# Moving the LayerNorm's scale and shift, and the weight rests, from GpSimd to VectorE in a two-block network

## The chip, the cores and the metric

The kernel runs on one core of a Trainium2 chip as one program with one launch. Its time is the time on the device in microseconds (us); lower is better. Before the change it is 3112.41 us, the median of three runs (3110.68 to 3112.63). A core has five engines that each work through their own queue in order: TensorE (PE in the profile; its weight loads are PEld), VectorE (DVE), ScalarE (ACT), GpSimd (POOL), and SyncE (SP), which issues most of the DMAs.

## The reference

512 tokens of 1024 channels pass through two blocks. The first, in which the change lies, has two layers, and each layer three sublayers, each closed by a LayerNorm over a residual sum:

```python
for l in range(DEPTH):                                  # DEPTH = 2
    h = 0.5 * _swiglu(x, ffn_w_gate[l, 0], ffn_w_up[l, 0], ffn_w_down[l, 0])
    x = _layernorm(ALPHA * x + h, ln_g[l, 0], ln_b[l, 0])
    h = _mixer(x, w_in[l], ...)
    x = _layernorm(ALPHA * x + h, ln_g[l, 1], ln_b[l, 1])
    h = 0.5 * _swiglu(x, ffn_w_gate[l, 1], ffn_w_up[l, 1], ffn_w_down[l, 1])
    x = _layernorm(ALPHA * x + h, ln_g[l, 2], ln_b[l, 2])
# _layernorm: (x - mean) * rsqrt(var + 1e-5) * g + b
# _swiglu:    (silu(x @ wg) * (x @ wu)) @ wd, width 2816
# _mixer:     x @ w_in, then a causal convolution of 31 taps with its own LayerNorm, a gated linear
#             recurrence, and attention in a window with a bias per relative position; then @ w_out
```

The second block (a state-space scan, a gating unit, and 16 routed experts) is not touched by the change.

## The kernel before, in words

**Numbers in split passes.** A product of two float32 matrices is made of three passes of a rounded type: high times high, high times low, low times high (`mm3`, lines 115 to 119). A weight unit of 128 x 1024 is therefore loaded into a ring of four raw buffers, rounded by ScalarE (line 82, tile `whl`), and its rest, raw minus rounded, is computed by a second engine (line 83). This document calls that instruction a rest. The ring of split units has seven places; a place comes free when TensorE has used its unit. Which engine computes a rest is told by `pool_lo`: in the three feed-forward stages after the first it is GpSimd for the first 6 units, in a mixer GpSimd for all 14 units of the input projection, and VectorE everywhere else.

**Stages.** The first block is six stages in a row, numbered from 0: feed-forward, mixer, feed-forward, and the same again. A stage projects its input (`proj`, 24 matmuls for 128 output columns), does its own work, and projects back in `down`. The tokens are four tiles `x[0]` to `x[3]` of 128 x 1024, and `down` works by halves of two tiles: the products of the second half lag five units behind those of the first, so that the LayerNorm of the first half can run beside the last products of the second.

**The boundary of two stages** is the end of `down` (lines 228 to 268). `ln_stats` forms the residual sum on VectorE (line 133), the squares and the root on ScalarE (lines 137 and 138), and normalizes on VectorE (line 141). The normalized tile is transposed by TensorE into PSUM (`transposes`, tile `tb`), and `evac_T` brings it back: ScalarE applies the LayerNorm's scale and shift, which on the transposed side are one number for each partition (line 160, tile `y`), VectorE rounds (line 162, tile `xTh`) and forms the rest (line 163, tile `xTl`). There are four such pairs for each half. Then TensorE projects the first four units of the next stage for the first half of the tokens (tile `pj`), with the transposes of `x[2]` and `x[3]` between them, and the next stage begins with the same units for the second half.

**The residual copy.** The tiles `x[t]` themselves, which the next LayerNorm needs again, are normalized but not yet scaled. `gb_apply` (lines 172 to 176) multiplies and adds on GpSimd with the scale and shift spread over all partitions (tile `gb`), two instructions for each tile, at the boundary. After the last stage another routine, `gb_halves`, does this, by halves on VectorE and GpSimd.

**The mixer** has VectorE run 62 taps of the convolution (tile `acc`, line 362), which are queued behind the projections' own work; the low part of each query (`ql`, line 396) is formed on the same engine, and TensorE needs it for the scores (`sc`, line 451). The bias band of the attention (tile `bias`) shares its one buffer with `gb`, and is loaded at the mixer's start by a DMA that GpSimd issues (line 610). GpSimd also does six products of the recurrence (lines 427 to 431).

**Order.** The program is written in one order, and a scheduler then orders each engine's queue by its own priorities and estimates. The places of instructions are told below from the built program.

Of the kernel before, what the change touches and what calls it, by code (L numbers as in the profile page):

```python
# [13 lines left out]
D = 1024  # L14
# [17 lines left out]
NPOOL = 6  # L32
# [7 lines left out]
class Stream:  # L40
    """Weight units, in the order the tensor engine takes them: loaded ahead into a ring,
    then (where a product runs in split passes) parted into a rounded and a rest."""
# [25 lines left out]
    def ensure(self, n):  # L68
        k = self.k
        while self.n_split < min(n, self.limit or len(self.units)):  # L70
# [6 lines left out]
            if self.units[i][1]:  # L77
                r = self.raw.pop(i)
                w = r.shape[-1]
                t = k.splitp.tile([128, 2, 1024], F32R, tag="hl", name="whl")  # L80
                hi, lo = t[:, 0, :w], t[:, 1, :w]
                k.nc.scalar.activation(hi, r, AF.Copy)  # L82
                k.lo_engine(i).tensor_tensor(out=lo, in0=r, in1=hi.bitcast(F32), op=OP.subtract)  # L83
                self.hl[i] = (hi, lo)
                self.load_to(i + 1 + RAWS)
# [14 lines left out]
class Kernel:  # L100
    def __init__(self, tc, a, out):
        self.tc, self.nc, self.a, self.out = tc, tc.nc, a, out
        self.bg = []

    def lo_engine(self, i):
        return self.nc.gpsimd if i in self.pool_lo else self.nc.vector

# [64 lines left out]
    def gb_apply(self, t):  # L172
        g, b = self.gb
        eng = self.nc.gpsimd
        eng.tensor_tensor(out=self.x[t], in0=self.x[t], in1=g, op=OP.mult)
        eng.tensor_tensor(out=self.x[t], in0=self.x[t], in1=b, op=OP.add)
# [20 lines left out]
    def down(self, u0, n, lhs, ln, nxt, at=None, pace=4):  # L197
        """lhs(u, half): the split stationary operand of unit u for a half of the tokens.
        nxt: a projection follows; its first units run for each half by itself."""
# [29 lines left out]
        g, b = self.ln_cols(ln)  # L229
        rest = [lhs(u, 1) for u in range(n - LAG, n)]  # L230
# [5 lines left out]
        for s in range(LAG):  # L236
# [5 lines left out]
            if s == LAG - TB:  # L242
                if nxt:
                    self.transposes(1, self.x[1], tb)
                    self.evac_T(0, tb, g, b)
                    self.gb_apply(0)
                    self.gb_apply(1)
# [10 lines left out]
        for i in range(4):  # L258
# [4 lines left out]
            if i == T3:  # L263
                self.transposes(3, self.x[3], tb)
                self.evac_T(1, tb, g, b)
                self.gb_apply(2)
                self.gb_apply(3)
# [7 lines left out]
    def ffn(self, st, pb, ln, nxt, setup=None, at=None, views=()):  # L275
# [4 lines left out]
        def post(f, pg, pu):  # L280
# [3 lines left out]
            nc.vector.scalar_tensor_tensor(h, sg, 0.5, pu, op0=OP.mult, op1=OP.mult)  # L284
            hs[f] = h

# [19 lines left out]
        for f in range(NF):  # L306
# [12 lines left out]
            post(f, pg, pu)  # L319
# [7 lines left out]
    def mixer(self, l, st, pb, ln, nxt):  # L327
# [26 lines left out]
        def tap(c, j):  # L354
            """Tap j of the causal convolution: its input reaches j tokens back."""
# [10 lines left out]
        def post_xb(c):  # L366
# [4 lines left out]
            for j in range(1, LTAPS):  # L371
                nc.vector.scalar_tensor_tensor(t[:, j:], b[:, :T - j], wj(j), t[:, j:], op0=OP.mult, op1=OP.add)
            xc.append(t)

# [169 lines left out]
        for c in range(2):  # L544
            pj(4 + c)
            post_xb(c)
        for c in range(2):
            pj(6 + c)
            self.drain(4)
        for c in range(2):  # L550
# [48 lines left out]
    def mixer_tiles(self, l, mp):  # L599
# [6 lines left out]
        self.kl = mp.tile([128, T], F32R, name="kl")  # L606
        self.bias = self.gbp.tile([128, 4, 2, 256], F32, tag="gb", name="bias")
# [9 lines left out]
    def setup(self):  # L617
# [9 lines left out]
        self.eps5 = self.cp1.tile([128, 1], F32, name="eps5")  # L627
# [9 lines left out]
    def lru_consts(self, pool):  # L637
        """8 log sigmoid(lambda) of each channel, and its negative."""
# [10 lines left out]
    def log1p_exp_neg_abs(self, pool, v, n):  # L649
        """log(1 + exp(-|v|)) by 2 atanh(e / (2 + e)), e = exp(-|v|)."""  # L650
# [17 lines left out]
    def band_bias(self, pool):  # L668
        """The additive band [query, r, g, key], -1e30 outside the window, from rel_bias."""
# [43 lines left out]
def chan(v, n):  # L713
    """[..., n*128] vectors as columns [128, ... * n]"""
# [4 lines left out]
def layout1(i):  # L719
# [9 lines left out]
    # natural q tile (2g + r//2), half r%2  ->  tile r holds (g, d)  # L729
# [44 lines left out]
class Carve:  # L774
    """Small tiles out of larger ones that are not in use yet."""
# [18 lines left out]
class Program(Kernel):  # L794
# [53 lines left out]
    def mod_cols(self):  # L848
        """shift and scale (lat, ctx) as columns; the scale with norm1's weight."""
# [38 lines left out]
    def xm_half(self, half, rs):  # L888
        """The modulated norm of two token tiles, transposed and split."""
# [17 lines left out]
    def ctx_stats(self):  # L907
        """The rms norm's factor of each token of the context, along a row, for all partitions."""
# [16 lines left out]
    def ctx_split(self):  # L925
        """The modulated norm of the context, transposed and split."""
# [22 lines left out]
    def proj2(self, i, bank, src, cols, every=0):  # L949
        """128 output channels for the columns cols of the split operand src."""  # L950
# [8 lines left out]
    def spread(self):  # L959
        """Some of the waiting steps, so that they end with the last of the places for them."""  # L960
# [62 lines left out]
    def conv3(self, bank, n, i, dst):  # L1023
        """Centred three-tap convolution with bias, then silu."""
# [8 lines left out]
    def grp_main(self, pool, g, u, ready={}):  # L1033
        """B, x (2 tiles) and C of a group: projection, convolution."""
# [27 lines left out]
    def grp_p1(self, pool, g, G):  # L1062
        """The states and the combined decay of a group, as steps to spread."""
# [60 lines left out]
        def step(dst, src, c, d, p):  # L1124
            """dst = src * chunk decay + state"""
# [115 lines left out]
    def norm_ss(self):  # L1241
        """The groups' rms norm of the scan's output."""
# [11 lines left out]
    def v_half(self, u, half):  # L1254
        """Natural projection of half of v's channels, with gelu, into the tokens' tiles."""
# [66 lines left out]
    def post(self, outer, U, xd):  # L1322
        nc, tc, w, a = self.nc, self.tc, self.w, self.a
        with ExitStack() as es:
# [86 lines left out]
            # h = x + merged @ (w_o * g1)  # L1411
# [583 lines left out]
```

## Time and profile before

| what | value |
|---|---|
| median of three runs | 3112.41 us |
| the profiled execution: span from first to last instruction | 3109.9 us |
| granted clock of TensorE over the span (1.0 is 2.4 GHz, 0.5 is 1.2 GHz) | 0.978 |
| TensorE busy | 2980.0 us, 96% |
| VectorE busy | 1347.5 us, 43% |
| ScalarE busy | 1000.7 us, 32% |
| GpSimd busy | 410.0 us, 13% |

The profile is one execution. A row of the timeline reads: start, duration, engine, line, operation, output and input with sizes, count, and in brackets how long the engine had stood idle and which engine and instruction it then had waited for. The rows give no time of their own for the run beside the span, which is 2.5 us under the median of the runs. The first block takes some 1960 us of the span, and its five boundaries lie at about 380, 587, 972, 1366 and 1574 us.

### The profile page before, as it was taken

To read this page: it belongs to the slowest core of one execution; us is meant where nothing else is said; L and a number is where in the kernel's file an instruction comes from. 1 tells how busy PE (TensorE), PEld (TensorE's weight loads), DVE (VectorE), ACT (ScalarE), POOL (GpSimd) and SP (SyncE) were. 2 spreads that over 40 slices of the span, in tenths; PEclk is the share of its full clock that TensorE was granted. 3 is DMA by queue.
4 is the path that set the end of the run, shared out by engine and by line. 5 is a ranking of instruction groups with operands and counts; after the bars stand their busy time and mean duration, and the time that the engine had idled before them with its cause. 6 is when DMAs were issued, how large, how long until landed. Compare 5 with 4: busy or idle time off the path is not lost.

```text
span 3109.9 us, 35375 instructions
## 1 busy us (share of the span) xinstructions
PE 2980.0 (96%) x14404; PEld 2241.7 (72%) x14404; DVE 1347.5 (43%) x2068; ACT 1000.7 (32%) x1583; POOL 410.0 (13%) x259
## 2 busy tenths in 40 slices
PE   8999998899998999989889999999999999999998
PEld 7888774788887878877578888878788884444443
DVE  4223468532335233357552234788773441211112
ACT  4223335322223222234543223577542221000002
POOL 0000341400004000053040000133230110000000
PEclk9999998899999999989999999999999999999999
DMA  6432324233322353222533323222433368999994
GB/s 192 113 95 82 95 78 153 88 106 98 95 77 87 106 192 106 81 84 70 167 115 95 95 82 97 90 95 82 139 127 95 95 252 330 360 379 379 379 369 176
DMA packets 127747, 465.91 MB, mean 150 GB/s; under 512 B 12901, under 2 KB 13429, under 8 KB 126560
## 3 DMA queue, kind: packets, MB, share of 16 engines
q1 hardware_dynamic: 119488, 435.81, 40.3%
q0 software_dynamic: 6656, 23.12, 2.6%
q10 hardware_dynamic: 1440, 4.72, 0.4%
q8 instruction: 113, 1.85, 0.3%
q14 instruction: 50, 0.41, 0.0%
HBM read 457.71 MB, written 5.88 MB: 149 GB/s over the span
## 4 chain that ended last, share of the span: by engine, by line
PE 84%; DVE 11%; DMA 2%; ACT 1%; POOL 1%; issue 1%; SPq 0%; DVEq 0%; ACTq 0%; POOLq 0%
PE dn L215 18%; PE pg L117 6%; PE pg L119 6%; PE pg L118 6%; PE pu L117 5%; PE pu L119 5%; PE pu L118 5%; PE ey L1674 4%; PE eg L1674 4%; PE eu L1674 4%; DVE acc L362 3%; PE pj L118 2%; PE ga L1661 2%; PE pj L119 2%; PE pj L117 2%; DVE xTl L163 2%
## 5 line engine op out<-in xcount | busy, mean ns | idle before, releaser
L83 DVE TENSOR_TENSOR whl<-raw,whl 128x1024 fp32r<-128x1024 f32 x339 | 430.5, 1274 | 669.0 <-ACT whl L82 668.2
L82 ACT ACTIVATE whl<-raw 128x1024 fp32r<-128x1024 f32 (+1 forms) x385 | 405.9, 1056 | 665.1 <-PE pu L119 238.1
L215 PE MATMUL dn<-whl,hhl 128*128 128x512 f32 x2112 | 495.0, 396 | 0.0
L215 PEld LDWEIGHTS dn<-whl,hhl 128*128 128x128 f32 x2112 | 396.6, 188 | 95.1
L117 PE MATMUL pg<-xTh,whl 128*128 128x512 f32 x768 | 300.2, 391 | 0.0
L119 PE MATMUL pg<-xTh,whl 128*128 128x512 f32 x768 | 299.0, 389 | 0.0
L118 PE MATMUL pg<-xTl,whl 128*128 128x512 f32 x768 | 298.9, 389 | 0.0
L117 PE MATMUL pu<-xTh,whl 128*128 128x512 f32 x704 | 274.6, 390 | 0.0
L119 PE MATMUL pu<-xTh,whl 128*128 128x512 f32 x704 | 273.9, 389 | 0.0
L118 PE MATMUL pu<-xTl,whl 128*128 128x512 f32 x704 | 273.9, 389 | 0.0
L118 PE MATMUL pj<-xTl,whl 128*128 128x256 f32 (+1 forms) x688 | 238.1, 346 | 32.2 <-DVE xTl L163 31.9
L117 PE MATMUL pj<-xTh,whl 128*128 128x256 f32 (+1 forms) x688 | 243.3, 354 | 21.7 <-DVE xTh L162 21.7
L83 POOL TENSOR_TENSOR whl<-raw,whl 128x1024 fp32r<-128x1024 f32 x46 | 113.1, 2465 | 925.7 <-ACT whl L82 925.6
L119 PE MATMUL pj<-xTh,whl 128*128 128x256 f32 (+1 forms) x688 | 233.9, 340 | 0.0
L118 PEld LDWEIGHTS pj<-xTl,whl 128*128 128x128 f32 x688 | 141.4, 206 | 49.1 <-DVE xTl L163 38.3
L117 PEld LDWEIGHTS pg<-xTh,whl 128*128 128x128 f32 x768 | 144.1, 188 | 36.6 <-issue 7.4
L117 PEld LDWEIGHTS pj<-xTh,whl 128*128 128x128 f32 x688 | 141.3, 205 | 36.3 <-DVE xTh L162 25.8
L119 PEld LDWEIGHTS pg<-xTh,whl 128*128 128x128 f32 x768 | 144.2, 188 | 30.0
L118 PEld LDWEIGHTS pg<-xTl,whl 128*128 128x128 f32 x768 | 144.3, 188 | 29.6
L1674 PE MATMUL eu<-er,xg 128*64 128x512 f32 x512 | 160.1, 594 | 0.0
L1674 PE MATMUL eg<-er,xg 128*64 128x512 f32 x512 | 152.9, 596 | 0.0
L119 PEld LDWEIGHTS pu<-xTh,whl 128*128 128x128 f32 x704 | 132.1, 188 | 27.7
(476 smaller groups left out, 4239.2 us busy)
## 6 DMA issues: line engine op xcount, KB each, us to landing
raw<-in_wgu SPq DMA_DIRECT2D x176, 512.0 KB, 3.5
er<-in_eu SPq DMA_DIRECT2D x64, 1024.0 KB, 10.0
er<-in_eg SPq DMA_DIRECT2D x64, 1024.0 KB, 9.8
er<-in_ed SPq DMA_DIRECT2D x56, 1024.0 KB, 7.4
raw<-in_wd SPq DMA_DIRECT2D x88, 512.0 KB, 3.5
raw<-in_win SPq DMA_DIRECT2D x76, 512.0 KB, 3.5
raw<-in_ada_w SPq DMA_DIRECT2D x48, 512.0 KB, 4.1
raw<-in_wout SPq DMA_DIRECT2D x16, 512.0 KB, 4.6
```

The lines of the kernel that those rows point to most:

```text
L82: k.nc.scalar.activation(hi, r, AF.Copy)
L83: k.lo_engine(i).tensor_tensor(out=lo, in0=r, in1=hi.bitcast(F32), op=OP.subtract)
L117: mm(out, l[0], r[0], start=start, stop=False)
L118: mm(out, l[0], r[1], start=False, stop=False)
L119: mm(out, l[1], r[0], start=False, stop=stop)
L163: nc.vector.tensor_tensor(out=lo, in0=y, in1=hi.bitcast(F32), op=OP.subtract)
L215: nc.tensor.matmul(banks[t, dh], l[:, s], r[:, dh * 512:(dh + 1) * 512], start=(u == 0 and n_l == 0), stop=(u == last and n_l == 2))
L362: nc.vector.scalar_tensor_tensor(acc[:, j:], y[:, :T - j], wj, acc[:, j:], op0=OP.mult, op1=OP.add)
L1661: nc.tensor.matmul(src, self.x[t][:, k * 128:k * 128 + 128], G[:, t], start=(t == 0), stop=(t == 3))
L1674: nc.tensor.matmul(banks[dh][r * 64:r * 64 + 64], l(k, r), ws[r][:, j, dh * 512:(dh + 1) * 512], start=(first and j == 0), stop=(last and ...
```

## The change

The scale and shift of the residual copy leave the boundary. `down` now only lists them, eight instructions for four tiles, and `gb_later` takes them from the list in the next stage and puts them on VectorE, each behind an instruction that it is given: in a feed-forward stage one for each step from the third, in a mixer two behind each of four places. All rests go to VectorE; `pool_lo` and `NPOOL` are gone. The bias band, which shares a buffer with the scale and shift, is loaded behind them. And a root of a one-number tile is placed in `down` ahead of the last part, so that ScalarE's table for the root is loaded there. Comments and docstrings were cut in the same edit, which moves line numbers only.

```diff
@@ Stream.ensure
-                k.lo_engine(i).tensor_tensor(out=lo, in0=r, in1=hi.bitcast(F32), op=OP.subtract)
+                k.nc.vector.tensor_tensor(out=lo, in0=r, in1=hi.bitcast(F32), op=OP.subtract)
...
-    def gb_apply(self, t):
-        g, b = self.gb
-        eng = self.nc.gpsimd
-        eng.tensor_tensor(out=self.x[t], in0=self.x[t], in1=g, op=OP.mult)
-        eng.tensor_tensor(out=self.x[t], in0=self.x[t], in1=b, op=OP.add)
+    def gb_later(self, n, ins):
+
+        with self.tc.issue_after(ins.ins):
+            for t, v, op in self.gb_todo[:n]:
+                self.nc.vector.tensor_tensor(out=self.x[t], in0=self.x[t], in1=v, op=op)
+        self.gb_todo = self.gb_todo[n:]
...
@@ down
         g, b = self.ln_cols(ln)
+        self.tc.keep_in_program_order(nc.scalar.activation(self.table, self.eps5, AF.Sqrt))
...
                     self.evac_T(0, tb, g, b)
-                    self.gb_apply(0)
-                    self.gb_apply(1)
...
                 self.evac_T(1, tb, g, b)
-                self.gb_apply(2)
-                self.gb_apply(3)
+        self.gb_todo = [(t, v, op) for t in range(4) for v, op in zip(self.gb, (OP.mult, OP.add))]
...
@@ ffn
-            post(f, pg, pu)
+            last = post(f, pg, pu)
+            if f >= 2:
+                self.gb_later(1, last)
...
@@ mixer
         for c in range(2):
             pj(4 + c)
-            post_xb(c)
+            last = post_xb(c)
+            self.gb_later(2, last)
         for c in range(2):
             pj(6 + c)
+            self.gb_later(2, last)
             self.drain(4)
+        self.load_band()
...
@@ run
-                self.pool_lo = set()
-                for st, us in self.u_in.items():
-                    self.pool_lo |= set(us[:14 if st % 3 == 1 else NPOOL if st else 0])
```

The built program's order shows three places. First VectorE at the boundary of stages 2 and 3, from the residual sum of the second tile (`x_67`) to the first pair of `evac_T`; before the change:

```order
L133 SCALAR_TENSOR_TENSOR x_67,st<-x_67,dn 128x512
L135 TENSOR_SCALAR st<-st 128x1
L140 RECIPROCAL st<-st 128x1
L141 TENSOR_SCALAR x_66<-x_66,st 128x1024
L140 RECIPROCAL st<-st 128x1
L141 TENSOR_SCALAR x_67<-x_67,st 128x1024
L162 CAST xTh<-y 128x2x256
L163 TENSOR_TENSOR xTl<-y,xTh 128x2x256
```

And the same stretch of VectorE's queue with the change:

```order
L130 SCALAR_TENSOR_TENSOR x_67,st<-x_67,dn 128x512
L132 TENSOR_SCALAR st<-st 128x1
L82 TENSOR_TENSOR whl<-raw,whl 128x1024
L137 RECIPROCAL st<-st 128x1
L138 TENSOR_SCALAR x_66<-x_66,st 128x1024
L137 RECIPROCAL st<-st 128x1
L138 TENSOR_SCALAR x_67<-x_67,st 128x1024
L82 TENSOR_TENSOR whl<-raw,whl 128x1024 x3
L159 CAST xTh<-y 128x2x256
L160 TENSOR_TENSOR xTl<-y,xTh 128x2x256
```

Four rests that stood on GpSimd now stand in this stretch, three of them right ahead of the first rounding; one more stands behind the residual sums of the second half.

The second place is VectorE in the mixer of stage 1, from the third low part of the queries (`ql`) to the first addition of the bias band (`S`); the number in `acc` rows is the length of a tap, which falls from 511 to 482 as the taps proceed. Before the change:

```order
L396 SCALAR_TENSOR_TENSOR ql<-pj,qh 128x512
L613 CAST xTh<-hs 128x512 x2
L614 TENSOR_TENSOR xTl<-hs,xTh 128x512 x2
L362 SCALAR_TENSOR_TENSOR acc<-yin,pc,acc 128x484
L362 SCALAR_TENSOR_TENSOR acc<-yin,pc,acc 128x483 x2
L362 SCALAR_TENSOR_TENSOR acc<-yin,pc,acc 128x482 x2
L396 SCALAR_TENSOR_TENSOR ql<-pj,qh 128x512
L458 ISA S,sm<-sc,bias,sinks 128x128
```

And with the change:

```order
L395 SCALAR_TENSOR_TENSOR ql<-pj,qh 128x512
L360 SCALAR_TENSOR_TENSOR acc<-yin,pc,acc 128x492
L360 SCALAR_TENSOR_TENSOR acc<-yin,pc,acc 128x491 x2
L360 SCALAR_TENSOR_TENSOR acc<-yin,pc,acc 128x490 x2
L360 SCALAR_TENSOR_TENSOR acc<-yin,pc,acc 128x489 x2
L618 CAST xTh<-hs 128x512
L395 SCALAR_TENSOR_TENSOR ql<-pj,qh 128x512
L619 TENSOR_TENSOR xTl<-hs,xTh 128x512
L618 CAST xTh<-hs 128x512
L360 SCALAR_TENSOR_TENSOR acc<-yin,pc,acc 128x488
L619 TENSOR_TENSOR xTl<-hs,xTh 128x512
L457 ISA S,sm<-sc,bias,sinks 128x128
```

Before, all taps stood ahead of the last `ql`; now the last 14 stand behind it.

The third place is GpSimd at the start of the first mixer, where `bias<-toep` is the load of the band; before the change:

```order
L176 TENSOR_TENSOR x_69<-x_69,gb 128x1024
L610 DMA bias<-toep 128x8x256
L83 TENSOR_TENSOR whl<-raw,whl 128x1024 x7
L427 TENSOR_TENSOR gate<-gate,xc 128x512 x2
L428 TENSOR_TENSOR gate<-gate,sq 128x512
L431 TENSOR_TENSOR hs<-hs,gl 128x512
```

And with the change, from the DMA ahead of it:

```order
L687 DMA toep<-bb 8x128x384
L615 DMA bias<-toep 128x8x256
L426 ISA
L426 TENSOR_TENSOR gate<-gate,xc 128x512 x2
L427 TENSOR_TENSOR gate<-gate,sq 128x512
L430 TENSOR_TENSOR hs<-hs,gl 128x512
```

GpSimd's products at the boundary are gone, the load of the band now waits for VectorE's last addition of the shift, and the `ISA` row, which before stood ahead of GpSimd's first rest in stage 0, stands behind that load.

## Rows read from the trace of the kernel before

**Rows 1.** Chain of work that ended last, shares of the span by engine.
```profile
PE 84%; DVE 11%; DMA 2%; ACT 1%; POOL 1%; issue 1%; SPq 0%; DVEq 0%; ACTq 0%; POOLq 0%
```

**Rows 2.** Waits of TensorE, whole span: us in total, times, longest us.
```profile
PE pj L118 <- DVE xTl L163: 31.9, 21, 2.4
PE pj L117 <- DVE xTh L162: 21.7, 17, 1.6
PE sc L451 <- DVE ql L396: 18.4, 4, 4.7
```

**Rows 3.** Busy time by stretch: five boundaries; length, engines, granted clock, DMA.
```profile
381.65:416.90 35.25, 23.10 (x137) 20.67 (x137) 26.45 (x28) 7.77 (x15) 22.68 (x10) 0.76 0.25 77
587.67:620.00 32.33, 22.30 (x136) 20.43 (x136) 25.55 (x29) 9.17 (x16) 20.57 (x10) 0.77 0.24 81
972.35:1004.70 32.35, 22.19 (x136) 20.40 (x136) 25.12 (x29) 9.16 (x16) 20.14 (x10) 0.79 0.26 80
1365.90:1400.60 34.70, 23.23 (x138) 21.04 (x137) 26.43 (x28) 7.78 (x15) 22.66 (x10) 0.75 0.26 77
1573.70:1605.80 32.10, 22.00 (x137) 20.13 (x137) 25.52 (x29) 9.17 (x16) 22.67 (x14) 0.79 0.24 71
```

**Rows 4.** Timeline of VectorE at the boundary of stages 2 and 3.
```profile
968.56 2.77 DVE L163 TENSOR_TENSOR xTl<-y,xTh 128x512 fp32r<-128x512 f32 x1
971.25 2.61 DVE L162 CAST xTh<-y 128x512 fp32r<-128x512 f32 x1
...
981.78 0.41 DVE L162 CAST xTh<-y 128x512 fp32r<-128x512 f32 x1
982.12 0.67 DVE L133 SCALAR_TENSOR_TENSOR x<-x,dn 128x512 f32<-128x512 f32 x1
...
982.72 0.68 DVE L163 TENSOR_TENSOR xTl<-y,xTh 128x512 fp32r<-128x512 f32 x1
...
985.27 1.22 DVE L83 TENSOR_TENSOR whl<-raw,whl 128x1024 fp32r<-128x1024 f32 x1
...
986.72 0.81 DVE L141 TENSOR_SCALAR x<-x,st 128x1024 f32<-128x1024 f32 x1
```

**Rows 5.** Timeline of GpSimd, same boundary.
```profile
978.79 2.52 POOL L83 TENSOR_TENSOR whl<-raw,whl 128x1024 fp32r<-128x1024 f32 x1
...
997.35 2.69 POOL L176 TENSOR_TENSOR x<-x,gb 128x1024 f32<-128x1024 f32 x1
```

**Rows 6.** Timeline of ScalarE, same boundary.
```profile
955.70 1.28 ACT L138 ACT_TABLE_LOAD   x1
...
965.91 1.06 ACT L82 ACTIVATE whl<-raw 128x1024 fp32r<-128x1024 f32 x1 [2.62 <-PE dn L215]
966.88 3.73 ACT L160 ACTIVATE y<-tb,pc 128x256 f32<-128x256 f32 x8
```

**Rows 7.** Timeline of TensorE, same boundary.
```profile
966.51 5.84 PE L215 MATMUL dn<-whl,hhl 128*128 128x512 f32 x24
...
992.51 1.03 PE L145 MATMUL tb<-ident,x 128*128 128x128 f32 x8
993.30 0.36 PE L117 MATMUL pj<-xTh,whl 128*128 128x256 f32 x1
...
996.13 0.28 PE L119 MATMUL pj<-xTh,whl 128*128 128x256 f32 x1
```

**Rows 8.** Timeline of VectorE in the mixer of stage 1.
```profile
439.63 2.23 DVE L362 SCALAR_TENSOR_TENSOR acc<-yin,pc,acc 128x511 f32<-128x511 f32 x1
...
485.55 4.52 DVE L362 SCALAR_TENSOR_TENSOR acc<-yin,pc,acc 128x487 f32<-128x487 f32 x7
...
495.62 0.68 DVE L396 SCALAR_TENSOR_TENSOR ql<-pj,qh 128x512 fp32r<-128x512 f32 x1
```

**Rows 9.** Timeline of GpSimd in stages 0 and 1.
```profile
361.46 2.40 POOL L83 TENSOR_TENSOR whl<-raw,whl 128x1024 fp32r<-128x1024 f32 x1 [298.86 <-ACT whl L82]
...
465.11 1.64 POOL L428 TENSOR_TENSOR gate<-gate,sq 128x512 f32<-128x512 f32 x1 [11.68 <-ACT sq L426]
```

**Rows 10.** DMA issues by line: queue, count, size, us to landing.
```profile
bias<-toep POOLq DMA_DIRECT2D x2, 1024.0 KB, 6.2
```

More of the change, by code (lines that the diff above doesn't have):

```diff
@@ L31 @@
 PER = 1
-NPOOL = 6
 ROWS = {1: (0,), 3: (1,), 4: (2,)}
@@ L103, in __init__ @@
         self.bg = []
-    def lo_engine(self, i):
-        return self.nc.gpsimd if i in self.pool_lo else self.nc.vector
+        self.gb_todo = []
     def ps(self, name="ps"):
@@ L283, in post @@
             h = views[f] if f < len(views) else self.hp.tile([128, 512], F32, tag="h", name="h", bufs=NF - len(views))
-            nc.vector.scalar_tensor_tensor(h, sg, 0.5, pu, op0=OP.mult, op1=OP.mult)
             hs[f] = h
+            return nc.vector.scalar_tensor_tensor(h, sg, 0.5, pu, op0=OP.mult, op1=OP.mult)
         split = {}
@@ L371, in post_xb @@
             for j in range(1, LTAPS):
-                nc.vector.scalar_tensor_tensor(t[:, j:], b[:, :T - j], wj(j), t[:, j:], op0=OP.mult, op1=OP.add)
+                ins = nc.vector.scalar_tensor_tensor(t[:, j:], b[:, :T - j], wj(j), t[:, j:], op0=OP.mult, op1=OP.add)
             xc.append(t)
+            return ins
         vn = []
@@ L606, in mixer_tiles, with load_band @@
         self.kl = mp.tile([128, T], F32R, name="kl")
+    def load_band(self):
+        nc = self.nc
         self.bias = self.gbp.tile([128, 4, 2, 256], F32, tag="gb", name="bias")
@@ L626, in setup @@
             self.w.load_to((1, 2, 2, RAWS)[t])
-        self.eps5 = self.cp1.tile([128, 1], F32, name="eps5")
+        eps = self.cp1.tile([128, 2], F32, name="eps5")
+        self.eps5, self.table = eps[:, 0:1], eps[:, 1:2]
         nc.vector.memset(self.eps5, LN_EPS)
```

## The prediction

> **What bounds the kernel now.** I read the chain that ended last first. TensorE carries 84% of the span and VectorE 11% [rows 1], so an edit on GpSimd can only pay where TensorE stands still. The list of TensorE's own waits says where that is: 31.9 us in 21 waits for the rest `xTl` and 21.7 us in 17 waits for the rounded `xTh`, all at the five boundaries of stages, and 18.4 us for the queries' low parts `ql`, in the two mixers [rows 2]. The boundaries are cut out by the same two events each time: from the end of the last product of the old stage to the 120th projection matmul of the new one (four units for the first half of the tokens, one for the second; 24 each). Together they take 35.25 + 32.33 + 32.35 + 34.70 + 32.10 = 166.73 us, at a granted clock of 0.75 to 0.79 [rows 3]: TensorE waits and, after its waits, runs partly at the lower of its two levels.
>
> Why it waits is seen on VectorE at the third boundary. One rounding takes 2.61 us and one rest 2.77 us, while the same instructions a few us on take 0.41 and 0.68 us [rows 4]. The reader should lay GpSimd's rows beside them: the last instruction of its first row of work ends at 978.79 + 2.52 = 981.31 us [rows 5], and the first short rounding starts at 981.78. In the second half it is the same again, until GpSimd's last addition ends at 1000.04. The slow instructions last as long as one of GpSimd's, 2.5 to 2.7 us.
>
> The Trainium skill, page "SBUF — State Buffer", section "SBUF: two separate sides", says that VectorE and GpSimd share one pair of ports, which an instruction of GpSimd holds for its whole length against an instruction of VectorE with two inputs in SBUF or in a fast mode. The trace agrees: 2.77 against 0.68 us. By that rule the slow instructions go when GpSimd's go, which the rows suggest without it.
>
> **The boundary with the change.** It removes from GpSimd, at each boundary, eight products of the residual copy and five or so rests, and adds four rests to VectorE ahead of the first pair and one more in the second half. I walk through the third boundary; time 0 is the end of the last product, 966.51 + 5.84 = 972.35 [rows 7].
>
> First half. ScalarE's scaled copies start at 966.88 and take 3.73 us for eight [rows 6]; TensorE was not late there, so this stays. VectorE must first do the rest of the unit that ScalarE rounds from 965.91 to 966.97 [rows 6]; at 1.22 us [rows 4] that ends at 968.2. Four pairs at 0.41 + 0.68 = 1.09 us end at 972.5. TensorE starts the projections at 972.35 and needs the fourth pair only after three pairs' worth of matmuls, 18 x 0.12 = 2.2 us later (from 993.30 to 996.13 lie 23 steps, 0.12 us each [rows 7]). No wait is left; before, the last pair was done at 983.4.
>
> Second half. From the first residual sum of `x[2]` to its normalized tile the old trace takes 982.12 to 986.72 + 0.81 = 987.53, 5.4 us with one rest in it [rows 4]. With one rest more it is 6.6 us, started when the fourth rounding is done, about 971.8: 978.4. Two projections, 48 x 0.12 = 5.8 us, bring TensorE to 978.1, so it waits 0.3 us. Then transposes (992.51 to 993.30, 0.79 us [rows 7]), a projection of 2.9, transposes, a projection: 985.8. The second half's four pairs follow ScalarE's copies, which start at about 982.3; the last is done near 987.7, when TensorE would need it at 985.8 + 2.2 = 988.0. The 120th matmul ends at 988.7. That is 16.3 us; I take 17.0 for restarts of the pipe that I cannot see. Bounds: 16.0 (120 x 0.12 + 2 x 0.79, no wait at all) and 22 (both chains late by a rest and a copy, 2.3 us each, with the clock falling again).
>
> The saving is 166.73 - 5 x 17.0 = 81.7 us; by the bounds 87 and 57.
>
> **The mixers.** VectorE's queue ends in the `ql` for which TensorE waits. Ahead of the last `ql` the change adds eight scale and shift instructions and three rests. No row has a scale or shift of 128 x 1024 on VectorE; the nearest is the rest, the same operation and size, 1.22 us [rows 4]: + 9.8 and + 3.7 us. It takes away 14 taps at 4.52 / 7 = 0.65 us [rows 8]: - 9.1 us. And three rests on GpSimd no longer collide with taps; one such tap took 2.23 us [rows 8], so - 3 x 1.6 = - 4.8 us. Sum - 0.4 us: the last `ql`, which ended at 496.3 [rows 8], moves little, and I count the mixers at 0. Bounds for both together: - 10 us (the gaps of VectorE's queue before the taps hide all the rests, and the TensorE wait of 9.2 us for each mixer [rows 2] halves) and + 16 us (the 14 taps, 9.1 us, come back in the scores, where VectorE also has the soft maximum to do).
>
> Queued behind the scale and shift is the band's load on GpSimd, and behind that GpSimd's `ISA` row and the six products of the recurrence. The load took 6.2 us to land [rows 10] and now starts some 40 us before the scores instead of 80. The `ISA` row has no duration in the trace; before, it lay in an idle time of 298.86 us [rows 9], so all that is known is that it takes less. In the first mixer it has about 11.68 us of GpSimd's idle time before the product that the scan needs [rows 9]. I count 0, and up to + 15 us once.
>
> **Counted at nothing.** In the feed-forward stages eight products of 1.22 us spread over eight steps lie on an engine that is 43% busy, under TensorE's steps of some 11 us; without that cover they would be 9.8 us a stage. The table load of 1.28 us [rows 6] was ahead of the first half's root, but TensorE ran on products until 972.35 without a gap, so taking it out of that chain gives 0, at most 1.3 us where a chain is late. SyncE's DMAs and their order are the same.
>
> **The sum.** 3109.9 (span) - 81.7 + 0 = 3028.2 us; the median of the runs lies 2.5 us over that span, so 3031 us.
>
> **Rivals.**
> *The rests hold the chain.* The third rest ahead of the first rounding waits for ScalarE, and ScalarE for a place that TensorE frees. If in the new order this is the last product, at 972.35, then rounding 1.06 and rest 1.22 put the first pair at 974.6 and its end at 979.0; TensorE loses about 4 us at each boundary and perhaps 5 in each mixer: 3031 + 20 + 10 = 3061 us. For it: VectorE takes its queue in order. Against: ScalarE's rounding of that unit started at 965.91 before [rows 6], and the copies still stand behind it.
>
> *The mixer pays.* The band comes late or the `ISA` row is long. If the load's landing comes 6.2 us after the last `ql`, each mixer loses 6 us, and 15 us once for the `ISA`: 3031 + 12 + 8 = 3051 us with half of the latter. For it: both now stand behind a busy VectorE. Against: some 40 us of slack.
> The same page of the Trainium skill warns that a load issued by GpSimd cannot write its descriptors while VectorE runs an instruction in a fast mode. In this trace the load landed in 6.2 us beside VectorE's roundings [rows 10]; no run here shows it beside the taps. It is the rule that would make this rival true, and its chance is in this case.
>
> *GpSimd is not the cause.* If the long roundings come from something else at the boundary (TensorE's or ScalarE's own traffic), they stay at 2.6 us, and the change only adds to VectorE: three rests ahead of the pairs (two of the four have room) and one behind, 4 x 1.22 = 4.9 us, and 9.1 us of taps in each mixer: 5 x 4.9 + 2 x 9 = 43 us, 3155 us. It decides against the change from the point where the roundings keep more than about 2.2 us. Against it: the switch from 2.6 to 0.41 us within half a us of GpSimd's end [rows 4, 5], twice at this boundary.
>
> *No change*: gains of the boundaries eaten by a later wait, such as weights that arrive too late. A unit of 512 KB is needed every 2.9 us only for four units that the ring has already, so I see nothing that would.
>
> **Chances.** Forecast 0.80 (3031, by itself 3016 to 3046), rests hold the chain 0.07 (3061), mixer pays 0.08 (3051), not GpSimd 0.03 (3155), no change 0.02. The range 3014 to 3058 leaves out the last two, a part of the second, and the forecast's own edge. About 0.2% (6 us) is what a measurement of this kernel can tell from no change; faster by more than that 0.95, within it 0.02, slower 0.03.
>
> **What would show it.** In the profile after: the rounding (`xTh`) and the rest (`xTl`) at the boundaries at 0.41 and 0.68 us throughout; TensorE's waits for them, 53.6 us now, under 6; the five stretches near 17 us at a clock near 1.0; GpSimd idle there; TensorE's wait for `ql` between 8 and 26 us. I am wrong if the roundings stay over 1 us, if a new wait of TensorE on `whl` or on `tb`'s inputs shows more than 2 us a boundary, or if the bias band appears as what VectorE waits for.

## The result and the profile after

The changed kernel takes 3023.19 us (median of 4 runs, 3022.63 to 3024.18) against 3111.83 us for the kernel before beside it (4 runs): a ratio of 0.9717, 95% interval 0.9705 to 0.9728. That is 88.6 us less; the forecast was 3031 us, in a range of 3014 to 3058. The profiled execution has a span of 3021.2 us and a mean granted clock of 0.992.

The chain that ended last reads by engine as before [rows 1]; the engine that bounds the kernel is the same. Shares of the span by engine, kernel after:

```profile
PE 84%; DVE 11%; ACT 1%; DMA 1%; issue 1%; POOL 1%; SPq 0%; DVEq 0%; ACTq 0%; POOLq 0%
```

TensorE's waits (us in total, times, longest) answer to [rows 2]; kernel after:

```profile
PE sc L450 <- DVE ql L395: 11.8, 4, 4.9
...
PE yv L495 <- ACT pT L490: 6.8, 3, 3.0
...
PE mod L840 <- DMA raw<-in_ada_w: 5.4, 5, 2.2
```

The two waits at the head of the list before, 31.9 us for `xTl` and 21.7 us for `xTh`, have no counterpart: no wait for these tiles at a boundary is left in the list. The five stretches, from the end of the old stage's last product to the 120th projection matmul, answer to [rows 3]. The columns are the stretch, its length, busy time (and instructions) of PE, PEld, DVE, ACT, POOL, granted clock, DMA share, GB/s. Kernel after:

```profile
381.68:398.13 16.45, 16.30 (x139) 16.12 (x138) 10.84 (x25) 7.89 (x15) 0.00 (x0) 1.00 0.27 81
567.81:584.38 16.57, 16.30 (x138) 16.13 (x138) 10.96 (x25) 9.17 (x16) 0.00 (x0) 1.00 0.20 64
935.61:952.06 16.45, 16.30 (x139) 16.12 (x138) 10.84 (x25) 9.17 (x16) 0.00 (x0) 1.00 0.22 65
1313.11:1329.56 16.45, 16.30 (x139) 16.12 (x138) 10.84 (x25) 7.89 (x15) 0.00 (x0) 1.00 0.25 81
1498.68:1515.26 16.58, 16.31 (x138) 16.14 (x138) 10.96 (x25) 9.17 (x16) 0.00 (x0) 1.00 0.21 64
sum 82.50, PE 81.50 PEld 80.63 DVE 54.43 ACT 43.29 POOL 0.00; mean PE 16.30 PEld 16.13 DVE 10.89 ACT 8.66 POOL 0.00
```

And the sum of the same five stretches in the kernel before, each taken to the modelled end of its 120th matmul:

```profile
sum 167.52, PE 113.62 PEld 103.46 DVE 129.08 ACT 43.06 POOL 108.73; mean PE 22.72 PEld 20.69 DVE 25.82 ACT 8.61 POOL 21.75
```

So the boundaries give back 167.5 - 82.5 = 85.0 of the 88.7 us of span. They did so in two ways. TensorE's idle time there fell from 167.5 - 113.6 = 53.9 us to 1.0 us, and the busy time of the same matmuls fell from 113.6 to 81.5 us, by 32.1 us. A reader who adds up only the waits finds 53 of the 85 us.

The 32.1 us have two parts. The granted clock was 0.75 to 0.79 before and is 1.00 after: where TensorE runs without a gap, the step from one matmul to the next was 0.153 us in the mean of the five stretches before and is 0.119 us now (in the third stretch before, 14 steps from 984.05 to 987.04 take 0.21 us each, and 22 from 993.50 to 996.13 take 0.12). Over some 635 steps that is about 22 us. And 40 matmuls stood just ahead of a wait: the next one started only after they had ended, so they count with 0.39 us each in place of a step, which makes up the other 10 us.

VectorE at the boundary of stages 2 and 3 answers to [rows 4]; the last product ends at 935.61. Kernel after:

```profile
930.27 1.23 DVE L82 TENSOR_TENSOR whl<-raw,whl 128x1024 fp32r<-128x1024 f32 x1 [2.46 <-ACT whl L81]
931.41 0.42 DVE L159 CAST xTh<-y 128x512 fp32r<-128x512 f32 x1
931.87 0.69 DVE L160 TENSOR_TENSOR xTl<-y,xTh 128x512 fp32r<-128x512 f32 x1
...
935.55 0.69 DVE L160 TENSOR_TENSOR xTl<-y,xTh 128x512 fp32r<-128x512 f32 x1
...
941.47 0.81 DVE L138 TENSOR_SCALAR x<-x,st 128x1024 f32<-128x1024 f32 x1
946.75 0.43 DVE L159 CAST xTh<-y 128x512 fp32r<-128x512 f32 x1 [4.47 <-ACT y L157]
...
950.40 0.69 DVE L160 TENSOR_TENSOR xTl<-y,xTh 128x512 fp32r<-128x512 f32 x1
```

All 40 roundings now take 0.42 to 0.43 us and all 40 rests 0.69 to 0.70 us. TensorE, in the same place, meets one wait of 0.15 us (answer to [rows 7]); kernel after:

```profile
941.50 1.07 PE L142 MATMUL tb<-ident,x 128*128 128x128 f32 x8 [0.15 <-DVE st L137]
```

### The profile page after: what moved, and what is told of

Same layout as the page of the kernel before. It is cut to its first block, busy times and chain, and to the rows that moved or that the text cites. A ratio compares the mean times of both kernels' runs of the same rounds, so it can differ in the third digit from the quotient of the medians.

```text
span 3021.2 us, 35336 instructions
## 1 busy us (share of the span) xinstructions
PE 2946.0 (98%) x14404; PEld 2216.2 (73%) x14404; DVE 1337.0 (44%) x2154; ACT 1002.0 (33%) x1589; POOL 190.3 (6%) x173
## 4 chain that ended last, share of the span: by engine, by line
PE 84%; DVE 11%; ACT 1%; DMA 1%; issue 1%; POOL 1%; SPq 0%; DVEq 0%; ACTq 0%; POOLq 0%
PE dn L213 18%; PE pg L114 6%; PE pg L116 6%; PE pg L115 6%; PE pu L114 5%; PE pu L116 5%; PE pu L115 5%; PE ey L1680 4%; PE eg L1680 4%; PE eu L1680 4%; DVE acc L360 3%; PE ga L1667 2%; PE pj L115 2%; PE pj L114 2%; PE pj L116 2%; PE wo L1442 1%
## 5 line engine op out<-in xcount | busy, mean ns | idle before, releaser
L82 DVE TENSOR_TENSOR whl<-raw,whl 128x1024 fp32r<-128x1024 f32 (+1 forms) x385 | 487.9, 1271 | 707.5 <-ACT whl L81 706.7
L114 PE MATMUL pj<-xTh,whl 128*128 128x256 f32 (+1 forms) x688 | 231.4, 336 | 0.0
L116 PE MATMUL pj<-xTh,whl 128*128 128x256 f32 (+1 forms) x688 | 224.5, 326 | 0.0
L115 PE MATMUL pj<-xTl,whl 128*128 128x256 f32 (+1 forms) x688 | 224.4, 326 | 0.0
L278 ACT ACTIVATE sg<-pg 128x512 f32<-128x512 f32 x80 | 47.7, 596 | 321.4 <-PE pg L116 321.4
L115 PEld LDWEIGHTS pu<-xTl,whl 128*128 128x128 f32 x704 | 132.2, 188 | 27.6 <-issue 0.2
L116 PEld LDWEIGHTS pu<-xTh,whl 128*128 128x128 f32 x704 | 132.2, 188 | 27.5
L114 PEld LDWEIGHTS pu<-xTh,whl 128*128 128x128 f32 x704 | 132.1, 188 | 27.5 <-ACT x L1277 0.2
```

What stands on the lines that cost most here:

```text
L82: k.nc.vector.tensor_tensor(out=lo, in0=r, in1=hi.bitcast(F32), op=OP.subtract)
L114: mm(out, l[0], r[0], start=start, stop=False)
L115: mm(out, l[0], r[1], start=False, stop=False)
L116: mm(out, l[1], r[0], start=False, stop=stop)
L278: nc.scalar.activation(sg, pg, AF.Silu)
```

## The experiments

Each kernel is a copy of the changed one with the edit that is shown, cut down to the lines that matter. I call the account of the prediction, by which VectorE's long instructions come from GpSimd's two-input instructions beside them, the contention theory.

Sum of the five stretches, the time from there to the end of the last product in the two mixers (stages 1 and 4), both read from one profile, and the time, all in us:

| kernel | five stretches | mixers | time | ratio to before (95%) |
|---|---|---|---|---|
| before | 167.5 | 170.6, 173.0 | 3111.83 | 1 |
| after | 82.5 | 169.7, 169.1 | 3023.19 | 0.9717 (0.9705 to 0.9728) |
| e1, rests on GpSimd | 100.5 | 174.9, 175.8 | 3051.66 | 0.9807 (0.9793 to 0.9820) |
| e2, scale and shift on GpSimd | 141.9 | 164.7, 165.2 | 3075.44 | 0.9882 (0.9869 to 0.9896) |
| e4, the same, asked for later | 141.6 | 167.5, 165.3 | 3075.18 | 0.9883 (0.9869 to 0.9896) |
| e12, the same, held back | 82.5 | 183.7, 182.7 | 3056.35 | 0.9820 (0.9803 to 0.9836) |
| e7, on VectorE at the boundary | 86.8 | 168.0, 165.7 | 3022.45 | one run |
| e5, two-input work added | 141.6 | 168.4, 169.2 | 3080.39 | one run |
| e6, one-input work added | 102.7 | 170.4, 169.4 | 3042.93 | one run |
| e3, no root ahead | 82.5 | 168.8, 169.1 | 3021.89 | 0.9714 (0.9700 to 0.9727) |
| e8, earlier in the mixer | 82.6 | 166.0, 171.6 | 3023.02 | 0.9719 (0.9706 to 0.9732) |
| e9, recurrence on VectorE | 82.5 | 168.6, 173.5 | 3025.53 | 0.9722 (0.9709 to 0.9736) |
| e10, e8 and e9 | 82.5 | 162.9, 165.6 | 3013.70 | 0.9684 (0.9671 to 0.9697) |
| e11, e10 and taps held | 82.5 | 163.6, 161.6 | 3009.43 | 0.9667 (0.9654 to 0.9680) |

### Is it GpSimd? Work added to the changed kernel (e5, e6)

```diff
+    def gb_apply(self, t):                      # called twice behind each evac_T, as before the change
+        for op in (OP.add, OP.subtract):        # e5
+            self.nc.gpsimd.tensor_tensor(out=self.x[t], in0=self.x[t], in1=self.gb[1], op=op)
+        for _ in range(2):                      # e6
+            self.nc.gpsimd.tensor_scalar(self.x[t], self.x[t], 1.0, None, op0=OP.mult)
```

> The changed kernel with eight more instructions on GpSimd at each boundary that nothing there needs: the shift is added to each tile of the residual copy and subtracted again, of the same size and operands as the scale and shift had. Contention theory: roundings and rests of the pairs take 2.5 to 2.8 us while they run, the five stretches are 26 to 30 us each, and the time is 3070 to 3090 us. Rival (not GpSimd): the stretches stay at 16.5 us, the time within 3 us of 3023.

It came out as the contention theory said. The third stretch, then GpSimd's first instructions and VectorE's row beside them; kernel e5:

```profile
958.24:986.24 28.00, 20.91 (x138) 19.61 (x138) 21.55 (x32) 9.17 (x16) 12.36 (x5) 0.88 0.14 44
```
```profile
949.04 11.57 POOL L171 TENSOR_TENSOR x<-x,gb 128x1024 f32<-128x1024 f32 x4 [242.78 <-PE tb L142]
```
```profile
955.78 2.63 DVE L159 CAST xTh<-y 128x512 fp32r<-128x512 f32 x1
958.44 2.72 DVE L160 TENSOR_TENSOR xTl<-y,xTh 128x512 fp32r<-128x512 f32 x1
961.09 0.42 DVE L159 CAST xTh<-y 128x512 fp32r<-128x512 f32 x1
```

GpSimd's four end at 949.04 + 11.57 = 960.61, and the next rounding takes 0.42 us. The instructions do nothing that the boundary needs, and 57 us are lost (one run). The rival that something else makes the roundings long is refuted.

> The same eight instructions more on GpSimd, but with one tensor as input (each tile multiplied by the number 1.0), at the same places. If any instruction of GpSimd holds VectorE back for its length: the pairs take as long as one of these, the stretches are over 22 us, 3050 to 3090 us by their length. If only instructions with two tensors do: roundings at 0.41 us and rests at 0.68 us beside them, 3023 to 3027 us.

Neither case. The stretch, GpSimd, VectorE; kernel e6:

```profile
944.03:964.28 20.25, 17.29 (x138) 16.30 (x138) 14.70 (x27) 9.18 (x16) 13.35 (x5) 1.00 0.15 53
```
```profile
953.09 11.48 POOL L171 TENSOR_SCALAR x<-x 128x1024 f32<-128x1024 f32 x4 [6.74 <-PE tb L142]
```

The last of these four by itself:

```profile
961.74 2.82 POOL L171 TENSOR_SCALAR x<-x 128x1024 f32<-128x1024 f32 x1
```
```profile
958.25 0.74 DVE L159 CAST xTh<-y 128x512 fp32r<-128x512 f32 x1
959.03 1.40 DVE L160 TENSOR_TENSOR xTl<-y,xTh 128x512 fp32r<-128x512 f32 x1
960.35 0.41 DVE L159 CAST xTh<-y 128x512 fp32r<-128x512 f32 x1
960.80 0.69 DVE L160 TENSOR_TENSOR xTl<-y,xTh 128x512 fp32r<-128x512 f32 x1
961.41 0.53 DVE L159 CAST xTh<-y 128x512 fp32r<-128x512 f32 x1
961.97 1.40 DVE L160 TENSOR_TENSOR xTl<-y,xTh 128x512 fp32r<-128x512 f32 x1
```

GpSimd is at least as busy as in e5 (13.35 us in the stretch against 12.36, and 2.87 us for each instruction), but every second rest takes 1.40 us and the others 0.69. The long ones stand where an instruction of GpSimd begins: the fourth begins at 961.74, during the rounding of 961.41 and just ahead of the rest of 961.97, while the pair before it, which runs wholly beside the third, takes the usual 0.41 and 0.69 us. The stretch is 3.8 us longer than after the change, at a clock of 1.00; the two-input work cost 11.6 us.

The Trainium skill, page "SBUF — State Buffer", section "SBUF: two separate sides", lets any instruction of GpSimd that reads SBUF and starts first hold the shared ports for its whole length against an instruction of VectorE with two inputs there. For two-input work of GpSimd the trace agrees (a rest of 2.72 us instead of 0.69); for one-input work it does not (a rest takes at most 1.40 us beside instructions of 2.87 us), and the measurement decides.

### Which part of the change? (e1, e2, e3)

```diff
# e1: the rests as before
-                k.nc.vector.tensor_tensor(out=lo, in0=r, in1=hi.bitcast(F32), op=OP.subtract)
+                k.lo_engine(i).tensor_tensor(out=lo, in0=r, in1=hi.bitcast(F32), op=OP.subtract)
# e2: the scale and shift as before, behind each evac_T, and none listed for later
+                    self.gb_apply(0)
+                    self.gb_apply(1)
# e3
-        self.tc.keep_in_program_order(nc.scalar.activation(self.table, self.eps5, AF.Sqrt))
```

> The changed kernel with the rests put back on GpSimd as they were before (six units in a feed-forward stage, fourteen in a mixer); the scale and shift stay on VectorE in the next stage. Contention theory: at a boundary GpSimd then still runs about 5 rests of 2.5 us (12.5 us) of the former 13 instructions (some 33 us), so about a third of the 16.8 us that each boundary lost comes back, 5 to 9 us each: 3023 + 25 to 45 = 3048 to 3068 us, roundings of 2.6 us wherever a rest of GpSimd runs and 0.41 us elsewhere. Rival (the scale and shift alone did it, by the length of their chain): 3023 to 3027 us and all five stretches near 16.5 us.

> The changed kernel with the scale and shift back on GpSimd at the boundary; all rests stay on VectorE. Contention theory: 8 instructions of 2.5 to 2.7 us, some 20 us of GpSimd at each boundary, bring back about two thirds of the 16.8 us, 10 to 13 us: 3023 + 50 to 65 = 3073 to 3088 us. Rival (the rests were what TensorE waited for, since they stood between the raw unit and the product): 3023 to 3030 us, the stretches near 17 us.

Both rivals fell, and both times lie where the theory had them, e1's by luck. At the boundaries the scale and shift on GpSimd cost 59.4 us, as expected, and the mixers, rid of these instructions, gave 8.9 us back. The rests cost 18.0, less than the 25 to 45 expected: with no scale and shift ahead of them on GpSimd, only one or two still run in a stretch. The sum, 77.4, is less than the 85.0 of both together. The rests cost more ahead of a mixer, where GpSimd had all 14, than ahead of a feed-forward stage; kernel e1:

```profile
381.28:403.75 22.47, 19.36 (x139) 18.66 (x138) 14.35 (x25) 7.77 (x15) 4.54 (x2) 0.85 0.20 60
...
948.72:967.41 18.69, 16.80 (x138) 16.23 (x138) 13.13 (x26) 9.17 (x16) 1.77 (x1) 1.00 0.19 59
```

What fills e1's time up to 3051.66 us was not in my expectation: in the mixers the rests on GpSimd cost 5.2 and 6.7 us more.

> The changed kernel without the root of a one-number tile ahead of the last part of the stage, so that the table load of 1.28 us stands in the first half's chain. Theory: TensorE has products until then and the last of the four pairs was 1.6 us ahead of its need, so + 0 to 0.3 us a boundary: 3023 to 3025 us. Rival (the chain is just in time): the load of 1.28 us shows in full at each of the five boundaries, + 6.4 us: 3029.6 us.

The ahead-loaded table is worth nothing that can be measured: the stretches are the same to 0.02 us.

### Engine or place? (e4, e12, e7)

```diff
# e4 and e12, in gb_later
-                self.nc.vector.tensor_tensor(out=self.x[t], in0=self.x[t], in1=v, op=op)
+                if op == OP.mult:     # e12 alone
+                    self.nc.vector.tensor_scalar(self.x[t][:, 0:1], self.x[t][:, 0:1], 1.0, None, op0=OP.mult)
+                self.nc.gpsimd.tensor_tensor(out=self.x[t], in0=self.x[t], in1=v, op=op)
# e7: as e2, with gb_apply on VectorE
+            self.nc.vector.tensor_tensor(out=self.x[t], in0=self.x[t], in1=v, op=op)
```

> The changed kernel with the scale and shift at the new places in the next stage, but on GpSimd instead of VectorE. Contention theory: the boundaries stay near 16.5 us, since GpSimd is idle there; in the feed-forward stages the slower VectorE is hidden; in a mixer eight instructions of 2.5 us slow taps by 8 x 1.6 = 13 us, against 9.8 us that VectorE no longer spends: + 3 us each, 3023 + 0 to 10 us. Rival (it is the engine that decides, wherever its work stands): 3060 us or more, with long roundings also outside the boundaries and TensorE waiting for them there.

My expectation missed because the kernel did not do what I meant: the stretches show GpSimd busy at the boundary. Kernel e4:

```profile
958.22:986.15 27.93, 20.59 (x139) 19.54 (x139) 21.57 (x32) 9.16 (x16) 13.55 (x7) 0.88 0.25 84
```

The order that `gb_later` asks for did not hold GpSimd. As I read it, on VectorE the instruction stands behind its step because other rows of VectorE's queue stand ahead of it; GpSimd's queue had none, and it began at 949.03, when TensorE's transposes (`tb`) had read its tile, 9.2 us ahead of the last product's end. e12 therefore holds it by data.

> The scale and shift on GpSimd in the next stage, this time held there: ahead of each product VectorE, in its own order behind the given instruction, multiplies one column of the tile by 1.0, and GpSimd needs that column. Theory (GpSimd's two-input instructions cost only where TensorE waits for VectorE): the boundaries at 16.5 us, the feed-forward stages as in the changed kernel, and in a mixer eight instructions of 2.6 us among the taps, which TensorE waits for, 5 to 12 us a mixer: 3023 + 10 to 24 = 3033 to 3047 us. Rival (GpSimd's work costs the same wherever it stands): 3070 us or more. Second rival (the place alone decides): 3020 to 3026 us.

The first theory's pattern, with the mixers mis-sized: they take 14.0 and 13.6 us more where I expected 5 to 12, and the time of 3056.35 us lies outside 3033 to 3047. The boundary, and what TensorE waited for over the span; kernel e12:

```profile
950.34:966.78 16.44, 16.29 (x138) 16.11 (x138) 10.83 (x25) 9.18 (x16) 0.00 (x0) 1.00 0.20 65
```
```profile
PE tv L390 <- ACT vT L384: 22.6, 2, 11.3
PE sc L452 <- DVE ql L397: 18.0, 4, 4.7
```

The boundaries are as after the change, and stages 2 and 3, in which GpSimd runs the eight instructions, take 351.2 and 361.0 us between boundaries, as after to 0.1 us. In the mixer GpSimd's 23 us of work slow the taps (four of them take 9.1 us from 425.06), and the recurrence, ScalarE and the transposed values (`vT`) come late behind them. The root that stands ahead of `vT` on ScalarE; kernel e12:

```profile
459.16 0.63 ACT L427 ACTIVATE sq<-sq 128x512 f32<-128x512 f32 x1 [18.25 <-DVE sq L426]
```

In the changed kernel that wait is 2.15 us. A further 7.5 us appear after the last boundary; in one wait of the second block (`rc` for `rm`) TensorE stands for 6.4 us, 2.1 in the changed kernel. I did not follow that.

> The scale and shift on VectorE, but at the boundary where they stood before, and not in the next stage. Theory: 4 x 1.22 = 4.9 us stand among the first half's pairs and ahead of the second half's residual sums, the same again in the second half; TensorE waits 4 to 9 us at each boundary, stretches of 20 to 25 us: 3023 + 20 to 45 = 3043 to 3068 us. Rival (only the engine matters, not the place): 3023 to 3028 us.

My theory fell. The stretch is only 0.7 to 1.1 us longer, and with the mixers free of these instructions (1.7 and 3.4 us less) the time of its one run is the same. Kernel e7:

```profile
936.35:953.51 17.16, 16.47 (x139) 16.17 (x138) 16.45 (x30) 9.18 (x16) 0.00 (x0) 1.00 0.28 93
```

VectorE is busy for 16.45 of 17.16 us; the scale and shift found room in the 4.5 us in which it otherwise waits for ScalarE's copies, and some stood ahead of the last product's end. So either half of the move, another engine or another place, clears the boundary; the place is not needed once the engine is VectorE, and GpSimd in the next stage pays in the mixers.

### What is left in the mixers (e8 to e11)

```diff
# e8: four behind each gated input of the convolution (post_conv), not behind post_xb
+                last = post_conv(i // 2); self.gb_later(4, last)
# e9: the recurrence's six products
-            nc.gpsimd.tensor_tensor(out=ig, in0=ig, in1=xc[c], op=OP.mult)      # and two more such lines
+            nc.vector.tensor_tensor(out=ig, in0=ig, in1=xc[c], op=OP.mult)
# e11: e8 and e9, drain(7) for drain(10) at the queries, and the taps left then behind the last ql
+            with self.tc.issue_after(last.ins): t()
```

> A candidate: in the mixer the eight scale and shift instructions are allowed four behind each gated input of the convolution, some 10 us earlier, where VectorE stands idle for about 9 us, instead of behind the recurrence's short convolutions. Theory (VectorE's queue ahead of the last low part of the queries is what TensorE waits for, 5.9 us a mixer): 3 to 5 us a mixer less, 3013 to 3018 us. Rival (the taps fill what is freed, or the rests behind these instructions come late): 3021 to 3026 us.

> A candidate: the six products of the recurrence in each mixer on VectorE instead of GpSimd. Contention theory: they cost 6 x 0.67 = 4.0 us of VectorE, and the taps beside them lose no more time (now about 6.5 us: 4.51 us for three taps, 4.36 to 4.39 us for five, instead of 0.67 each): 0 to 3 us a mixer less, 3017 to 3023 us. Rival (VectorE is simply given more work): 4 us a mixer more, 3031 us.

> Both candidates: scale and shift earlier in the mixer, the recurrence's products on VectorE. Theory: the two add, 4 to 8 us a mixer, as far as TensorE's waits for the queries go (5.9 us a mixer): 3009 to 3016 us. Rival: the taps that the scheduler puts ahead of the last query take it back, 3019 to 3024 us.

> The same with 26 of the 62 taps held behind the last low part of the queries by an explicit order (now 14 stand behind it). Theory: the wait for the queries goes altogether (5.9 us a mixer), and the taps find room in the scores: 3008 to 3013 us. Rival (the taps, 12 x 0.66 = 8 us more behind the queries, come late for the convolution's LayerNorm or hold back the soft maximum): 3020 to 3030 us, TensorE waiting for pT or in the last part of the mixer.

Alone, neither helps: 3023.02 us, as e8's rival had it, and 3025.53 us, between e9's theory and its rival. In e8 54 taps stand ahead of the last `ql` instead of 48. In e9 the wait for `ql` is gone and others stand in its place. TensorE's waits in the second mixer; kernel e8, then e9:

```profile
PE sc L451 <- DVE ql L396: 4.9, 2, 4.5
PE dn L213 <- DVE ab L849: 3.6, 1, 3.6
PE tp L486 <- DVE S L474: 2.9, 1, 2.9
```
```profile
PE mod L840 <- DMA raw<-in_ada_w: 5.0, 2, 3.1
PE sc L450 <- DVE sm L457: 3.3, 1, 3.3
```

Together they give 9.5 us, and holding 26 taps behind the last query 4.3 more (no run of e11 is as slow as the fastest of e10, 3012.19 us); both lie where their theories had them. Why the two together give what neither does alone is read from the waits only. Kernel e10, then e11, second mixer:

```profile
PE mod L840 <- DMA raw<-in_ada_w: 3.3, 4, 1.4
PE yv L496 <- ACT pT L491: 3.2, 2, 2.8
```
```profile
PE mod L844 <- DMA raw<-in_ada_w: 2.4, 3, 1.1
PE yv L496 <- DVE sm L462: 2.3, 1, 2.3
```

e11, 3009.43 us (3006.04 to 3010.04), is the fastest kernel here, 13.8 us under the changed one.

## Why the prediction was right

**The cause: right.** GpSimd's two-input instructions made the roundings and rests long; e5 puts eight such instructions back at each boundary and nothing else, and the stretches return to 28 to 29 us. The signs named beforehand came: roundings and rests short throughout, no wait for them at a boundary, GpSimd idle in the stretches, the clock at 1.00, and 11.8 us of waiting for `ql`.

**The boundary: right, by its own steps.** The four pairs of the first half were to end 0.15 us after the last product and ended 935.55 + 0.69 - 935.61 = 0.63 us after it. The second half's tile was to be ready at + 6.05 with a wait of 0.3; its transposes started at + 5.89 after a wait of 0.15. Its last pair was to end at + 15.35 and ended at + 15.48; the stretch was worked out as 16.3 and is 16.45. The 17.0 that I then took, 0.7 us a stretch for restarts of the pipe, is the mis-sized part; no run shows that term. 85.0 us came back, not 81.7: 2.5 of the 3.3 us are this, and 0.8 come from ending the stretches before with the modelled end of the 120th matmul (167.5 us) and not as in [rows 3] (166.7).

**The rests do not hold the chain.** The order lists three rests ahead of the first rounding, but the last of them ends at 931.50, 4.1 us before the last product; that rival is refuted.

**The mixers: inside the bounds, but not the 0 that I chose.** They gave 0.9 and 3.9 us. VectorE from the boundary's end to the last `ql` of the first mixer took 79.2 us before and 75.6 after. Groups of that stretch (line, names, shapes, count, busy us and mean ns, idle time before them), kernel before:

```profile
L362 DVE SCALAR_TENSOR_TENSOR acc<-yin,pc,acc 128x511 f32<-128x511 f32 (+29 forms) x60 | 49.0, 882 | 0.0
L372 DVE SCALAR_TENSOR_TENSOR xc<-pj,pc,xc 128x511 f32<-128x511 f32 (+2 forms) x6 | 4.5, 746 | 6.3 <-ACT xc L370 6.3
...
L351 DVE TENSOR_TENSOR yin<-pj,sg 128x512 f32<-128x512 f32 x2 | 1.4, 692 | 10.5 <-ACT sg L350 10.5
```

And with the change:

```profile
L360 DVE SCALAR_TENSOR_TENSOR acc<-yin,pc,acc 128x511 f32<-128x511 f32 (+22 forms) x46 | 36.9, 861 | 0.0
L173 DVE TENSOR_TENSOR x<-x,gb 128x1024 f32<-128x1024 f32 x8 | 9.5, 1215 | 0.0
L82 DVE TENSOR_TENSOR whl<-raw,whl 128x1024 fp32r<-128x1024 f32 x7 | 8.5, 1219 | 3.8 <-ACT whl L81 3.8
L370 DVE SCALAR_TENSOR_TENSOR xc<-pj,pc,xc 128x511 f32<-128x511 f32 (+2 forms) x6 | 4.5, 743 | 3.5 <-ACT xc L368 3.5
...
L349 DVE TENSOR_TENSOR yin<-pj,sg 128x512 f32<-128x512 f32 x2 | 1.4, 692 | 2.4 <-ACT sg L348 2.4
```

The scale and shift cost 9.5 us as estimated (9.8). The rests were seven, not three: 8.5 us against 3.7. The taps ahead of it fell by 12.1 us, where I had 9.1 for fourteen fewer and 4.8 for collisions. What closed the sum is the cover that I had left to the bounds: idle time fell from 16.8 to 9.7 us; some 2 us more are in smaller rows. So the change of - 0.4 us that I had worked out came near the - 3.7 us measured partly by luck: I had the rests 4.8 us too low and the taps' saving 1.8 us too high, and had left out 7.1 us of cover. Of the 3.7 us only 0.9 reached the end of the first mixer: TensorE's wait for `ql` fell there from 9.2 to 6.0 us, but its wait for `pT` rose from 2.9 to 4.7, and 0.8 us for `S` are new. The rival in which the mixer pays fell too: GpSimd issues the band's load at 430.79, 45 us before the first addition of the band at 475.80, the loads land after 6.2 us in the median as before, now beside the taps, and the `ISA` row fits into the 0.1 us between that issue and the next product. GpSimd, kernel after:

```profile
430.79 0.93 POOL L615 DMA_DIRECT2D bias<-toep  x1 [368.15 <-DVE x L173]
431.82 2.55 POOL L426 TENSOR_TENSOR gate<-gate,xc 128x512 f32<-128x512 f32 x2
```

**Counted at nothing: right.** Stages 2 and 3 take 351.2 and 361.1 us between boundaries, 352.2 and 361.0 before, with the eight instructions in them; the table is e3.

**The sum.** 85.0 (boundaries) + 4.8 (mixers) + 0.9 (stage 2) - 2.0 (behind the last boundary: 1504.0 us before, 1505.9 after) = 88.7 us. Of the 2.0 us, 1.2 are one wait of TensorE in the second block (`rc` for `rm`, 0.9 us before and 2.1 after); why it grew stays open, and the kernels tried have 1504.8 to 1508.3 there, e12 apart. Against the forecast's span of 3028.2 us the kernel is 7.0 us faster: 3.3 at the boundaries, 4.8 in the mixers and 0.9 in stage 2, less the 2.0.

## What to carry to other kernels

Before moving work off an engine, read how long its neighbours' instructions take beside it: one rounding of 2.6 us next to others of 0.4 pointed at the cause, and the engine that was slowed, not the one that was busy, set the price. A wait of TensorE can cost more than its own length, here 85 us for 53 us of idle time, because the matmuls around it ran at a lower granted clock and the one just ahead of it counted in full. An order asked for with one engine's queue in mind held nothing on another engine here (e4); look in the trace whether the moved work has moved, and test place and engine apart.

## What the runs showed of the hardware that was not expected

A one-input instruction of GpSimd (128x1024, 2.87 us) lengthens one rounding and rest of VectorE, those at its start, by 0.8 to 1.3 us in all (from 0.53 + 1.40 to 1.02 + 1.40 instead of 0.42 + 0.69), where beside two-input ones of the same size each rounding or rest takes up to 2.6 to 2.8 us. In e6 TensorE stood idle for 20.25 - 17.29 = 3.0 us of the stretch and its granted clock stayed at 1.00; in e1, in the first stretch, it stood idle for 3.1 us and the clock was 0.85, so the idle time of a stretch alone did not tell what the clock would do. The waits lay differently: e1's three between 2.4 and 6.1 us after the last product, e6's five spread from 2.7 to 19.4 us after it. No run shows whether that decided it.
